# A three-tile pool of their own for the sums of a Strassen block's weights

## The chip, the cores and the metric

The kernel runs on one core of one Trainium2 chip. The metric is the device time of one execution in microseconds (us), lower is better. A core has a matrix engine (TensorE, PE in the profile, with its weight loads as PEld), a vector engine (VectorE, DVE), an activation engine (ScalarE, ACT), a general engine (GpSimd, POOL) and a queue engine that issues transfers (SyncE, SP). The engines run their own instruction streams in order and wait for each other by semaphores.

## The reference, cut to what matters

One layer of a decoder runs over 512 prompt positions and 8 x 4 sample positions, 544 columns in all. It ends in a feed-forward part, and the change concerns that part alone:

```
h2 = _rmsnorm(x, norm2_g) * (1 + sc2) + sh2
u1, u2 = jnp.split(h2 @ w_up, 2, axis=-1)          # w_up: 1024 x (2 x 2816)
x = x + g2 * ((jax.nn.silu(u1) * u2) @ w_down)     # w_down: 2816 x 1024
```

All values are float32. The part ahead of it (gated linear attention, windowed attention, gates and an output projection) is unchanged in what it computes.

## The kernel before

Activations lie feature by feature: a tile is 128 features x 544 columns (half a tile, 272 columns, is one matmul's width). A float32 product is made of three matmuls: each operand is split into a high part (a cast, on ACT) and a low part (the difference, on DVE), and the program sums hi*hi, hi*lo and lo*hi.

**Memory.** Almost every tile is taken from one pool, `heap`, of 62 slots of 128 x 544 floats. When a tile is no longer used, its slot goes back; the next tile takes a slot that was given back earlier, and its first writer waits until the slot's last users are done. Weights arrive by SP's queue in pieces of 128 x 2048 (`raw`, three buffers) and are split into pairs of 128 x 1024 tiles (`hi`, `lo`, three buffers each). `heap2` is a pool of 14 further slots that is opened when the feed-forward part starts, for the low and high parts of the operand sums TC below.

**The feed-forward part.** The program fixes each engine's order as it is written (there is no scheduler). The 22 output blocks of `w_up` (a u1 and a u2 block of 128 columns each) are made in two ways. Blocks 0 to 2 are plain products (`fm_pair`, L498). Blocks 3 to 21 are Strassen-Winograd products: seven products of half size, w1 to w7, in place of eight. They need

- sums of activations, once: `combos` (L1756), called for q = 0 to 3. Each makes four vector sums (L1761 on POOL, L1762, L1764 and L1766 on DVE) and splits them (`split`, L518: cast L521 on ACT, difference L522 on DVE) into the TC tiles;
- sums of weights, for each block: `s_sums` (L1779). POOL adds and subtracts the four 128 x 512 quarters of the block's `raw` piece in four instructions, L1784 to L1787, and leaves three sums in tiles S[0], S[1], S[2]; the fourth result is written over a quarter of `raw`. Below, "the sums of block n" are these four instructions.

The weights are then split by `s_pair` (cast L1796 on ACT, difference L1797 on DVE): `s_a` splits two raw quarters (for w1, w2), `s_b` splits S[0] and S[1] (w5, w6), `s_c` splits S[2] and the changed quarter (w3, w7), and `s_d` (L1813) the last quarter (w4, L1817 and L1818). `s_run` (L1849) goes through the blocks in three groups. The groups are blocks 3 to 8, 9 to 16 and 17 to 21. While block n's products run on PE in the order w2, w5, w6, w3, w7, then block n+1's w1 (`s_first`), then n's w4, the next block's weights are prepared, in this order: `s_sums(n+1)` ahead of everything, `s_a(n+1)` behind w2, `s_d(n)` behind w5, `s_b(n+1)` behind w6, `s_c(n+1)` behind w7. Each product has 12 matmuls (L1831). w4 is summed onto the same PSUM bank as w7 and may only start when DVE has read w7's result (L1876).

Ahead of the first group, `ffn` (L1888) interleaves the plain products of blocks 0 to 2 with the four `combos` and calls `s_sums(3)`. Behind each group stands the product with `w_down` (`down`).

Of the kernel before, what the change touches and what calls it, by code (L numbers as in the profile page):

```python
# [6 lines left out]
F32 = mybir.dt.float32  # L7
# [49 lines left out]
def ffn_order():  # L57
    seq = []
    f = 3
    for i, g in enumerate(GROUPS):  # L60
        top = min(g[-1] + 1, KF - 1)
        while f <= top:
            seq.append(("S", f))
            f += 1
        seq.append(("D", i))
    return seq
# [15 lines left out]
def prep(inp):  # L82
# [7 lines left out]
    def slab(w):  # L90
        k, n = w.shape
        return w.reshape(k // 128, 128, n).transpose(1, 0, 2).reshape(128, -1)
# [28 lines left out]
    for kind, i in ffn_order():  # L121
        if kind == "S":
            a1, a2 = slab(up("u1", i)), slab(up("u2", i))
# [205 lines left out]
class Body:  # L329
# [278 lines left out]
    def run(self):  # L608
        nc, tc, I, O = self.nc, self.tc, self.I, self.O
        with ExitStack() as es:  # L610
            P = lambda **k: es.enter_context(tc.tile_pool(**k))
            self.cp = P(name="const", bufs=1)
            self.sm = P(name="small", bufs=2)
            self.heap = P(name="heap", bufs=62)
            self.rawp = P(name="rawp", bufs=3)
            self.hip = P(name="hip", bufs=3)
            es.enter_context(tc.manual_schedule())
            with ExitStack() as em:
                Q = lambda **k: em.enter_context(tc.tile_pool(**k))
                self.kvp = Q(name="kvp", bufs=2)  # L620
                self.cm = Q(name="cmid", bufs=1)
                self.startup()
                with ExitStack() as ep:
                    self.psd = ep.enter_context(tc.tile_pool(name="psd", bufs=4, space=PSUM))
                    self.pmm = ep.enter_context(tc.tile_pool(name="pmm", bufs=2, space=PSUM))
                    self.mixers()
                    self.mid()
                self.psd = P(name="psf", bufs=8, space=PSUM)
                self.pmm = None
            self.heap2 = P(name="heap2", bufs=14)  # L630
            self.nheap2 = 14
            self.ffn()

    def startup(self):
# [205 lines left out]
    def gla_head(self, hd):  # L840
# [26 lines left out]
        v = lambda j: self.v[hd // 2][j][:, 256 * (hd % 2):256 * (hd % 2) + 256]  # L867
        S = {}
        us = [self.sd(), self.sd()]
        st = [self.t2("S"), self.t2("S")]  # L870
        o = lambda j: slice(256 * (j % 2), 256 * (j % 2) + 256)
        for j in range(4):
            nc.tensor.matmul(us[j // 2][:, o(j)], lhsT=klt[:, 128 * j:128 * j + 128], rhs=v(j), start=True, stop=True)
        for j in range(4):
# [3 lines left out]
            else:  # L878
                nc.vector.scalar_tensor_tensor(out=t, in0=S[j], scalar=self.fac[:, hd, 0, 2 * j:2 * j + 1],
                                               in1=u, op0=ALU.mult, op1=ALU.add)  # L880
            S[j + 1] = t
        self.store(self.O["sp"][hd], S[4], 2)
# [896 lines left out]
    def s_sums(self, n):  # L1779
        nc = self.nc  # L1780
        raw = self.s_raw(n)
        seg = [raw[:, 512 * i:512 * i + 512] for i in range(4)]
        S = [self.t2("S")[:, :512] for _ in range(3)]
        nc.gpsimd.tensor_add(S[0], seg[0], seg[3])  # L1784
        nc.gpsimd.tensor_sub(S[1], S[0], seg[1])
        nc.gpsimd.tensor_sub(seg[0], seg[1], seg[0])
        nc.gpsimd.tensor_sub(S[2], seg[2], S[1])  # L1787
        self.S[n] = S
# [53 lines left out]
    def s_first(self, n):  # L1842
# [4 lines left out]
        self.open[n] = (a, c, t)  # L1847

    def s_run(self, run, after):  # L1849

        nc = self.nc
        for n, nxt in zip(run, run[1:] + [None]):
            if nxt:
                self.s_sums(nxt)
# [33 lines left out]
    def ffn(self):  # L1888
# [76 lines left out]
        for j, (run, g) in enumerate(runs):  # L1965
            self.pos += 16 * len(run)

            def after():
                self.nchunk = self.pos // 8
                self.w_split(self.nchunk)  # L1970

            self.s_run(run, after)
            if j + 1 < len(runs):
                self.down(g, runs[j + 1][0][0])
            else:
                self.h2 = self.TC = None
                self.down_last(g)
# [113 lines left out]
```

## Time and profile before

| what | value |
|---|---|
| time, median of three runs | 1056.63 us (1056.44 to 1057.69) |
| the profiled execution's own time, its span | 1055.36 us, 1053.6 us |
| PE busy | 1014.9 us (96% of the span) |
| DVE, ACT, POOL busy | 580.4, 424.9, 269.7 us |
| DMA, mean share of 16 engines, read and written | 45% in the large queue, 143.8 and 36.6 MB |

The span runs from the first to the last instruction of the profiled execution; 1.8 us of its time lie outside. PE is the engine that has least idle time, so what counts is where PE waits, and for whom. The feed-forward part begins at about 650 us. In the kernel's views, "idle before" or a number in square brackets is the time that an engine waited ahead of an instruction and the instruction that released it.

### The profile page before, as it was taken

What the parts mean: (1) busy time and instruction counts of PE and PEld (TensorE: products, weight loads), DVE (VectorE), ACT (ScalarE), POOL (GpSimd) and SP (SyncE); (2) the same over time, 40 slices, a digit from 0 to 9 for tenths busy, and PEclk for the clock granted to TensorE, in tenths of its full rate; (3) what the DMA queues carried; (4) which work ended last, traced back from release to release, by engine and by line L of the source; (5) the groups of instructions that cost most, each with busy time, mean ns of one, the idle gap of its engine ahead of it and who ended that gap; (6) DMA issues with size and microseconds to landing.
All of it is one profiled execution on the core that took longest, in us unless ns stands there. A gap on an engine that the chain in (4) does not pass through costs nothing.

```text
span 1053.6 us, 21620 instructions
## 1 busy us (share of the span) xinstructions
PE 1014.9 (96%) x9309; PEld 954.5 (91%) x9309; DVE 580.4 (55%) x950; ACT 424.9 (40%) x728; POOL 269.7 (26%) x272
## 2 busy tenths in 40 slices
PE   8999999999999999999999999979999999999996
PEld 6898789999889999998989999879999999999995
DVE  6654424433452476353225767888734897447755
ACT  5452114554426422632043335455521655215553
POOL 0103004442332000200011431826114452044112
PEclk9999999999999999999999999989999999999997
DMA  9846572432133427725886572124473332322202
GB/s 366 329 137 254 204 269 98 176 128 85 59 116 118 161 91 264 270 81 168 294 295 219 187 212 108 41 91 159 169 302 140 141 120 81 121 80 81 90 32 85
DMA packets 47991, 169.21 MB, mean 161 GB/s; under 512 B 4044, under 2 KB 26924, under 8 KB 32412
## 3 DMA queue, kind: packets, MB, share of 16 engines
q1 hardware_dynamic: 47208, 166.90, 44.7%
q8 instruction: 73, 1.20, 0.5%
q10 hardware_dynamic: 688, 0.93, 0.3%
q14 instruction: 22, 0.18, 0.1%
HBM read 143.76 MB, written 36.63 MB: 171 GB/s over the span
## 4 chain that ended last, share of the span: by engine, by line
PE 85%; DVE 8%; ACT 3%; issue 3%; DMA 1%; POOL 1%; DVEq 0%; ACTq 0%; POOLq 0%
PE sd L1831 16%; PE mm L492 11%; PE mm L496 10%; PE mm L494 10%; PE sd L492 4%; PE sd L494 4%; PE sd L496 4%; PE mm L1026 3%; PE mm L1028 2%; PE mm L1027 2%; DVE lo L1797 2%; PE sd L538 2%; PE sd L1005 1%; PE sd L1406 1%; DVE lo L440 1%
## 5 line engine op out<-in xcount | busy, mean ns | idle before, releaser
L492 PE MATMUL mm<-hh,hi 128*128 128x272 f32 x656 | 139.3, 294 | 1.4 <-DVE gk L762 1.1
L496 PE MATMUL mm<-hh,lo 128*128 128x272 f32 x656 | 136.1, 289 | 1.2 <-DVE lo L440 1.2
L494 PE MATMUL mm<-hl,hi 128*128 128x272 f32 x656 | 135.7, 288 | 0.0
L440 DVE TENSOR_TENSOR lo<-raw,hi 128x1024 fp32r<-128x1024 f32 x92 | 115.1, 1252 | 35.7 <-ACT hi L439 35.3
L439 ACT CAST hi<-raw 128x1024 fp32r<-128x1024 f32 x92 | 95.3, 1046 | 76.6 <-PE sd L494 45.3
L492 PEld LDWEIGHTS mm<-hh,hi 128*128 128x128 f32 x656 | 102.7, 188 | 7.8 <-issue 3.1
L496 PEld LDWEIGHTS mm<-hh,lo 128*128 128x128 f32 x656 | 102.7, 188 | 1.5 <-DVE lo L440 1.4
L494 PEld LDWEIGHTS mm<-hl,hi 128*128 128x128 f32 x656 | 103.1, 189 | 0.0
L1784 POOL TENSOR_TENSOR S<-raw 128x512 f32<-128x512 f32 x19 | 29.0, 1529 | 188.6 <-DMA raw<-in_wst_dram 127.2
L1831 PE MATMUL sd<-h2h,hi 128*128 128x272 f32 x228 | 66.7, 292 | 5.5 <-ACT hi L1796 5.5
L1831 PE MATMUL sd<-h2h,lo 128*128 128x272 f32 x228 | 66.5, 292 | 0.4 <-DVE lo L1797 0.4
L1831 PE MATMUL sd<-h2l,hi 128*128 128x272 f32 x228 | 66.3, 291 | 0.0
L1831 PE MATMUL sd<-tch,lo 128*128 128x272 f32 x228 | 65.7, 288 | 0.0
L1831 PE MATMUL sd<-tcl,hi 128*128 128x272 f32 x228 | 65.5, 287 | 0.0
L1831 PE MATMUL sd<-tch,hi 128*128 128x272 f32 x228 | 65.4, 287 | 0.0
L492 PE MATMUL sd<-acth,hi 128*128 128x272 f32 x304 | 63.0, 288 | 0.0
L494 PE MATMUL sd<-actl,hi 128*128 128x272 f32 x304 | 62.8, 288 | 0.0
L496 PE MATMUL sd<-acth,lo 128*128 128x272 f32 x304 | 62.8, 288 | 0.0
L1099 ACT ACTIVATE qs<-mm,ca 32x544 f32<-32x544 f32 x48 | 33.9, 706 | 59.2 <-PE mm L496 53.9
L1470 ACT ACTIVATE sg<-mm,ca 128x544 f32<-128x544 f32 x16 | 11.4, 715 | 100.9 <-PE mm L496 92.4
L1797 DVE TENSOR_TENSOR lo<-S,hi 128x512 fp32r<-128x512 f32 x57 | 45.1, 820 | 9.9 <-ACT hi L1796 9.2
L1026 PE MATMUL mm<-hi,hh 128*128 128x512 f32 (+1 forms) x128 | 49.0, 383 | 0.0
(390 smaller groups left out, 2634.6 us busy)
## 6 DMA issues: line engine op xcount, KB each, us to landing
raw<-in_wst_dram SPq DMA_DIRECT2D x70, 1024.0 KB, 5.0
ada<-in_wada_dram SPq DMA_DIRECT2D x24, 1024.0 KB, 8.1
out_rest_dram<-in_rest_dram SPq DMA_DIRECT2D x16, 768.0 KB, 7.5
out_kn_dram<-kg SPq DMA_DIRECT2D x5, 1024.0 KB, 6.0
x<-in_xT_dram SPq DMA_DIRECT2D x16, 272.0 KB, 5.0
kg<-in_kg_dram SPq DMA_DIRECT2D x4, 1032.0 KB, 9.3
s<-in_s_dram SPq DMA_DIRECT2D x4, 1024.0 KB, 5.3
vg<-in_vg_dram SPq DMA_DIRECT2D x4, 1024.0 KB, 5.4
```

The costliest lines, as they stand in the source:

```text
L439: self.nc.scalar.copy(hi, src)
L440: self.nc.vector.tensor_sub(lo, src, hi)
L492: nc.tensor.matmul(outs[h], lhsT=wh, rhs=xh[:, h * NH:(h + 1) * NH], start=first, stop=False)
L494: nc.tensor.matmul(outs[h], lhsT=wh, rhs=xl[:, h * NH:(h + 1) * NH], start=False, stop=False)
L496: nc.tensor.matmul(outs[h], lhsT=wl, rhs=xh[:, h * NH:(h + 1) * NH], start=False, stop=last)
L538: nc.tensor.matmul(pa[32 * j:32 * j + 32, :64].rearrange("p (t i) -> p t i", t=2), lhsT=self.csil[:, 32 * k:32 * k + 32], rhs=wk[:, :, j, ...
L1026: nc.tensor.matmul(out(tt), lhsT=xh, rhs=wh, start=(k == 0), stop=False)
L1027: nc.tensor.matmul(out(tt), lhsT=xh, rhs=wl, start=False, stop=False)
L1099: nc.scalar.activation(self.two(qs)[32 * q:32 * q + 32], ps[32 * s:32 * s + 32, :, :NH], AF.Identity, bias=b[32 * s:32 * s + 32])
L1784: nc.gpsimd.tensor_add(S[0], seg[0], seg[3])
L1797: self.nc.vector.tensor_sub(lo[:, c:c + w], s, hi[:, c:c + w])
L1831: nc.tensor.matmul(out, lhsT=a[:, w], rhs=b, start=first and k == 0 and j == 0, stop=last and k == 3 and j == 2, skip_group_check=True)
```

## The change

The S tiles no longer come from `heap`. A pool `spool` with three tiles of 128 x 512 is opened with the feed-forward part, and `s_sums` takes S[0], S[1], S[2] from it for each block. To make room, `heap` has 61 slots in place of 62, and `heap2` 12 in place of 14, so that the last two sums of `combos`, rather than the last one, are split into `heap` tiles.

```diff
-            self.heap = P(name="heap", bufs=62)
+            self.heap = P(name="heap", bufs=61)
...
-            self.heap2 = P(name="heap2", bufs=14)
-            self.nheap2 = 14
+            self.spool = P(name="spool", bufs=3)
+            self.heap2 = P(name="heap2", bufs=12)
+            self.nheap2 = 12
...
-        S = [self.t2("S")[:, :512] for _ in range(3)]
+        S = [self.spool.tile([128, 512], F32, tag="S", name="S_%d" % self.bump()) for _ in range(3)]
```

On all five engines the instructions stand in the same order as before, and they do the same work; line numbers from L630 on are one higher. What differs is what some of them wait for. On POOL these are the sums of blocks 3, 4 and 5 before, each with the semaphores that it waits for (PE_49, DVE_49, Pool_49 count the instructions done on an engine, the DMAHW ones transfers landed):

```order
L1784 TENSOR_TENSOR S_7741<-raw_7515 128x512 [waits DMAHW0_49,PE_49]
L1785 TENSOR_TENSOR S_7742<-S_7741,raw_7515 128x512 [waits PE_49,Pool_49]
L1786 TENSOR_TENSOR raw_7515<-raw_7515 128x512 [waits DMAHW5_49]
L1787 TENSOR_TENSOR S_7743<-raw_7515,S_7742 128x512 [waits DVE_49,Pool_49]
L1784 TENSOR_TENSOR S_7788<-raw_7786 128x512 [waits DMAHW1_49,PE_49]
L1785 TENSOR_TENSOR S_7789<-S_7788,raw_7786 128x512 [waits PE_49,Pool_49]
L1786 TENSOR_TENSOR raw_7786<-raw_7786 128x512 [waits DMAHW6_49,DVE_49]
L1787 TENSOR_TENSOR S_7790<-raw_7786,S_7789 128x512 [waits PE_49,Pool_49]
L1784 TENSOR_TENSOR S_7925<-raw_7833 128x512 [waits DMAHW2_49,DVE_49]
L1785 TENSOR_TENSOR S_7926<-S_7925,raw_7833 128x512 [waits DVE_49,Pool_49]
L1786 TENSOR_TENSOR raw_7833<-raw_7833 128x512 [waits DMAHW7_49,DMAHW4_49,DVE_49]
L1787 TENSOR_TENSOR S_7927<-raw_7833,S_7926 128x512 [waits DVE_49,Pool_49]
```

And the same twelve of the changed kernel:

```order
L1785 TENSOR_TENSOR S_7744<-raw_7518 128x512 [waits DMAHW0_49]
L1786 TENSOR_TENSOR S_7745<-S_7744,raw_7518 128x512 [waits Pool_49]
L1787 TENSOR_TENSOR raw_7518<-raw_7518 128x512 [waits DMAHW5_49]
L1788 TENSOR_TENSOR S_7746<-raw_7518,S_7745 128x512 [waits Pool_49]
L1785 TENSOR_TENSOR S_7791<-raw_7789 128x512 [waits DMAHW1_49,DVE_49]
L1786 TENSOR_TENSOR S_7792<-S_7791,raw_7789 128x512 [waits DVE_49,Pool_49]
L1787 TENSOR_TENSOR raw_7789<-raw_7789 128x512 [waits DMAHW6_49]
L1788 TENSOR_TENSOR S_7793<-raw_7789,S_7792 128x512 [waits DVE_49,Pool_49]
L1785 TENSOR_TENSOR S_7928<-raw_7836 128x512 [waits DMAHW2_49,DVE_49]
L1786 TENSOR_TENSOR S_7929<-S_7928,raw_7836 128x512 [waits DVE_49,Pool_49]
L1787 TENSOR_TENSOR raw_7836<-raw_7836 128x512 [waits DMAHW7_49,DMAHW4_49]
L1788 TENSOR_TENSOR S_7930<-raw_7836,S_7929 128x512 [waits DVE_49,Pool_49]
```

Before, block 4's sums waited for matmuls, the last users of the heap slots that they got. Now the wait of the sum S[i] of block n+1 on DVE is for the difference (L1797, now L1798) of block n's S[i], the last reader of the same buffer: S[0] and S[1] follow `s_b(n)`, S[2] follows `s_c(n)`. For block 3 there is nothing to wait for but its transfer.

## Rows read from the trace of the kernel before

**Rows 1.** Waits of PE from 640 us on: total, times, longest.

```profile
PE sd L1831 <- ACT hi L1796: 5.5, 1, 5.5
PE sd L1831 <- DVE u L1876: 4.6, 6, 1.0
...
PE sd L492 <- ACT hi L439: 1.3, 1, 1.3
PE sd L496 <- DVE lo L440: 1.0, 1, 1.0
```

**Rows 2.** PE in order of time: start, us, operation, [idle before it].

```profile
697.44 0.59 PE L1831 MATMUL sd<-h2h,hi 128*128 128x272 f32 x1 [5.49 <-ACT hi L1796]
...
710.42 0.29 PE L1831 MATMUL sd<-tch,wh 128*128 128x272 f32 x1
...
732.79 0.39 PE L1831 MATMUL sd<-tch,wh 128*128 128x272 f32 x1 [0.99 <-DVE u L1876]
```

**Rows 3.** ACT in order of time, a cast of 128x1024.

```profile
681.79 1.04 ACT L439 CAST hi<-raw 128x1024 fp32r<-128x1024 f32 x1
```

**Rows 4.** DVE in order of time, 677 to 696 us.

```profile
677.22 1.55 DVE L522 TENSOR_TENSOR tcl<-ta,tch 128x544 fp32r<-128x544 f32 x1 [0.18 <-ACT tch L521]
678.70 1.81 DVE L522 TENSOR_TENSOR tcl<-tb,tch 128x544 fp32r<-128x544 f32 x1
...
681.91 1.56 DVE L522 TENSOR_TENSOR actl<-su,acth 128x544 fp32r<-128x544 f32 x1 [0.71 <-ACT acth L521]
683.39 1.21 DVE L440 TENSOR_TENSOR lo<-raw,hi 128x1024 fp32r<-128x1024 f32 x1
...
686.78 0.72 DVE L522 TENSOR_TENSOR tcl<-tb,tch 128x544 fp32r<-128x544 f32 x1
687.42 0.50 DVE L1762 SCALAR_TENSOR_TENSOR tb<-h,dB,h 128x272 f32<-128x272 f32 x1
...
689.68 1.81 DVE L522 TENSOR_TENSOR tcl<-tb,tch 128x544 fp32r<-128x544 f32 x1
691.42 1.50 DVE L1762 SCALAR_TENSOR_TENSOR tb<-h,dB,h 128x272 f32<-128x272 f32 x1
...
694.38 1.39 DVE L1766 SCALAR_TENSOR_TENSOR tb<-h,B,ta 128x272 f32<-128x272 f32 x1
```

**Rows 5.** POOL in order of time: block 4's first sum, block 5's first and last.

```profile
676.90 1.29 POOL L1784 TENSOR_TENSOR S<-raw 128x512 f32<-128x512 f32 x1 [0.70 <-DMA raw<-in_wst_dram]
...
689.60 1.31 POOL L1784 TENSOR_TENSOR S<-raw 128x512 f32<-128x512 f32 x1 [6.71 <-DMA raw<-in_wst_dram]
...
694.01 1.46 POOL L1787 TENSOR_TENSOR S<-raw,S 128x512 f32<-128x512 f32 x1
```

**Rows 6.** DVE in order of time, block 3 of the first group.

```profile
702.31 1.90 DVE L1797 TENSOR_TENSOR lo<-S,hi 128x512 fp32r<-128x512 f32 x3 [1.53 <-ACT hi L1796]
...
707.37 1.29 DVE L1797 TENSOR_TENSOR lo<-S,hi 128x512 fp32r<-128x512 f32 x2 [0.47 <-ACT hi L1796]
...
709.11 0.44 DVE L1876 TENSOR_TENSOR u<-sd,s 128x272 f32<-128x272 f32 x1
```

**Rows 7.** Groups of DVE instructions from 640 us: count, busy us, mean ns.

```profile
L1859 DVE TENSOR_TENSOR su<-sd,sA 128x272 f32<-128x272 f32 x19 | 8.2, 430 | 0.0
```

**Rows 8.** Busy time by stretch: PE, PEld, DVE, ACT, POOL, granted clock, DMA.

```profile
694.80:701.70 6.90, 3.82 (x15) 3.50 (x16) 4.97 (x7) 2.78 (x6) 0.67 (x1) 0.51 0.00 0
```

**Rows 9.** DVE in order of time, during block 12's products.

```profile
854.10 2.38 DVE L1797 TENSOR_TENSOR lo<-S,hi 128x512 fp32r<-128x512 f32 x2
```

**Rows 10.** POOL in order of time, beside rows 9.

```profile
848.36 1.30 POOL L1784 TENSOR_TENSOR S<-raw 128x512 f32<-128x512 f32 x1 [3.92 <-DVE lo L1797]
...
853.58 1.74 POOL L1787 TENSOR_TENSOR S<-raw,S 128x512 f32<-128x512 f32 x1
```

**Rows 11.** The pm tiles: loads and readers, count, ns, first to last start.

```profile
L367 SPq DMA_DIRECT2D pm<-in_cb_dram x2: 328/534/741, 434.9 to 443.5; - x2
L1365 DVE TENSOR_TENSOR pn<-pm,sd x2: 677/680/682, 458.7 to 459.3; 96x512 f32<-96x512 f32 x2
```

## Prediction

> **What bounds the kernel now.** PE is busy for 96% of the span, so a change can gain only where PE waits. I read the waits of PE from the feed-forward part on first: one wait of 5.5 us for a cast of ACT (L1796), six of 4.6 us together for L1876 on DVE, and two smaller ones for the split of a chunk (L439, L440) [rows 1]. In order of time the long one stands at 697.44, ahead of w1 of block 3, the first Strassen product; the longest of the six stands at 732.79, ahead of w4 of block 5 [rows 2].
>
> Then I follow the long wait back. The cast that ends it has the shape of the one at 681.79, which takes 1.04 us [rows 3], so it begins at about 696.4. On ACT it stands behind the casts of the last `combos`, which need the sums that DVE makes between 689.68 and 695.77 (694.38 + 1.39). What to see there is DVE's own durations: the same split (L522, 128x544) takes 0.72 at 686.78 and 1.81 at 689.68, the same sum (L1762) 0.50 at 687.42 and 1.50 at 691.42; the row left out behind it is a second sum of 1.50 [rows 4]. POOL's rows say why: block 5's four sums run from 689.60 to 695.47, block 4's four from 676.90 on [rows 5]. A DVE instruction that reads two SBUF tiles ends 0.3 to 0.6 us after the POOL instruction under way (678.77 after 678.19) [rows 4, 5]. So PE waits for a chain on DVE and ACT, and sums on POOL that nobody needs for another 10 us lengthen that chain.
>
> **The change, part by part.**
>
> *Block 4's and 5's sums move.* With three S tiles, block 4's first sum waits for the difference of block 3's S[0], the first of the three at 702.31, which lies behind w1 of block 3; block 5's waits for block 4's, at 707.37 [rows 6]. Both leave the stretch ahead of 697.44. What DVE gets back, by rows of the same shape without POOL beside them: 677.22, 678.70 and 681.91 lose 0.83, 1.09 and 0.84, together 2.76; 689.68 loses 1.09, and the three sums of 128x272 behind it 1.00, 1.00 and 0.89, together 3.98 [rows 4].
>
> How much of it arrives at 697.44? The difference at 683.39 also needs its cast. With DVE 1.92 earlier, the cast begins at 681.79 - 1.92 = 679.87, ends at 680.9, and the difference follows, 2.4 earlier than before [rows 3, 4]. I take 2.4 of the 2.76. From there DVE and ACT alternate up to 689 without a wait for PE or a transfer, so the 2.4 is carried; the 3.98 is added in full, since ACT's casts stand directly behind these sums. PE then begins block 3 at 697.44 - 6.4 = 691.0. Its plain products ended at 691.95 (697.44 - 5.49) [rows 2]; of their own waits of 1.3 and 1.0 for that chunk [rows 1] at least 1.7 goes, so they end by 690.3 and are no new bound. Term: **-6.4**. Bounds: -4.0 (the first part is lost) and -6.7 (all of both).
>
> *The granted clock.* Behind the long wait the granted clock is 0.51 from 694.8 to 701.7, the lower of the two levels (1.2 GHz) [rows 8]. PE works in 4.3 us of that; at the upper level it would need at most 2.1 less. The wait that is left is about 3 us, still long, so I keep the cost: term 0, bounds -2.1 and +1.0.
>
> *What is given back.* Block 4's sums now run from about 702.99 - 6.4 = 696.6 on, beside DVE's work for block 3: the differences of S[1], S[2], of raw pieces, and of block 4's S[0] and S[1]. The trace has no sums of POOL there, so I price it by its nearest rows: each of the four POOL instructions holds back one difference by up to 1.09, 4.4 in all [rows 4]. Who waits is L1876 of block 3, which is queued behind them on DVE; w4 may not start ahead of it. DVE has 0.47 idle at 707.37, and L1876 ends at 709.55 [rows 6], 0.87 before PE comes to w4 at 710.42 [rows 2]. So PE loses 4.4 - 0.5 - 0.9 = 3.0. Bounds: 0 (POOL gets its turn only in DVE's gaps) and 6.4 (the whole gain). Term: **+3.0**.
>
> Here it matters which DVE instructions are held back. L1859, L1873 and L1876 read one operand from PSUM. L1859 stands right ahead of a long difference, in the stretch where POOL adds; its 19 have a mean of 430 ns and 8.2 us together [rows 7], so none is long. The Trainium skill says the same ("SBUF — State Buffer", section "Who interferes with whom"): a VectorE instruction with at most one SBUF input does not contend with GpSimd, one with two does, and the later one waits for the whole of the other. The trace agrees with both halves. If PSUM readers were held back too, L1873 and L1876 would cost another 2.2 at block 3.
>
> *The other blocks.* Sixteen blocks have a successor in their group. Before, POOL is two blocks ahead: it adds when a raw piece has landed, for instance from 848.36 to 855.32 [rows 10], right beside `s_b`'s pair of differences, which takes 2.38 at 854.10 [rows 9] against 1.29 at 707.37 [rows 6]. L1876 stands behind that pair. Afterwards POOL begins when S[0]'s difference is done, so that this pair and what stands ahead of it on DVE run free, 1.1 us earlier or more, and POOL meets what stands behind: L1877, S[2]'s difference, the changed quarter's, the next `act`. PE needs none of these within the next product. So I expect the waits of w4 for L1876 inside a group to go: three of the six (the 0.99 at 732.79 stands for them [rows 2]). The other three stand at the last block of a group, where no w1 lies between w7 and w4, and stay. Three of 0.8 to 1.0 are about 2.5; I take **-2.0**, bounds -2.6 and 0. The sums stay in time: the next block needs them a block later, 10.7 us (two blocks lie between 710.42 and 732.79, less the 0.99 [rows 2]), and four take 5.9 to 7.0 [rows 5, 10].
>
> *One heap slot and two slots of `heap2` fewer.* No instruction is added; a tile gets a slot that was given back one tile later. The longest delay that I find is SP's first pm load: issued at 434.9, it may have to wait as long as the second, to 443.5. Nothing is queued between the two, and they are read at 458.7, 15 us on [rows 11]; without that cover the 8.6 would be paid. Term 0, bounds 0 and +1.
>
> Sum: -6.4 + 3.0 - 2.0 = **-5.4**. Against the profiled execution's own 1055.36 that is 1050.0; the runs have a median 1.27 above it, so the forecast is 1056.63 - 5.4 = **1051.2 us**.
>
> **Rivals.**
>
> *Cleaner:* nothing is given back, and the clock stays up after the shorter wait: -6.4 - 2.1 - 2.0, 1046.1. For it: DVE issues back to back there. Against: POOL got its turn between DVE's instructions in every stretch shown. Chance 0.13.
>
> *Given back at once:* block 4's sums, made late, also hold up `s_b(4)`. The pair that reads S[0] and S[1] begins at 707.37 - 6.4 = 701.0 [rows 6], its cast some 0.5 earlier (half of the 1.04 [rows 3]), at 700.5; the two sums, begun at 696.6, need 3.0 to 3.5. With 0.4 to 0.9 of slack it can happen; the whole 6.4 may go, and only the -2.0 counts: 1054.6 to 1056.6. Chance 0.11.
>
> *Slower, three tiles are too few:* every block's sums wait for the differences of the block before. If the four, taking turns with DVE, needed over 13 us in place of 7, each of the 16 would be late for `s_c` and PE would wait for the excess; at 0.5 us each that is +8, less the 3.4 that the start keeps: 1061. The trace speaks against it by a factor of two [rows 10]. The Trainium skill has the rule that speaks for it ("Perfetto Trace Analysis", section "Optimization Strategy"): a gap that repeats on the engine that should be saturated can mean too few buffers. No run here shows such a gap on PE yet. Chance 0.07.
>
> *The change does nothing:* the cast ahead of 697.44 is held by something that comes just behind DVE. The rows show no such thing, and ACT's work there is short. Chance 0.03, within 1 us of before.
>
> **How the numbers follow.** The forecast has 0.66; its own range is 1048.5 to 1054. A difference below 0.2% (2.1 us) is about what a measurement of this kernel can't tell from none. Faster: 0.66, 0.13 and a third of the 0.11: 0.83. Same: the rest of the 0.11 and the 0.03: 0.10. Slower: 0.07. The range for 8 in 10 leaves out half of the cleaner case, the slower one and the upper end of the second: 1047.0 to 1056.0.
>
> **What would show it.** POOL: no sums between 677 and 696, block 4's first right behind block 3's S[0] difference. DVE: L522 at 0.72 and L1762 to L1766 at 0.50 in the last `combos`. PE: idle ahead of block 3 near 3 us, not 5.49; a new wait of 2 to 4 us for L1876 at w4 of block 3; no wait inside groups. It would be wrong if DVE's rows were long there without POOL beside them, if ACT's L1796 waited for POOL in each block, or if L1876 took longer than 0.44.

## The result, and the profile after

| what | before | after |
|---|---|---|
| time, median of four runs | 1056.76 us (1056.44 to 1057.69) | 1045.58 us (1044.85 to 1046.29) |
| ratio, 95% interval | | 0.9898 (0.9883 to 0.9912) |
| profiled execution, its span | 1055.36, 1053.6 us | 1045.04, 1043.3 us |
| PE busy | 1014.9 us (96%) | 1011.5 us (97%) |

The change gains 11.2 us where 5.4 were forecast; five more runs gave 0.9902 (0.9885 to 0.9919). The two profiles of the changed kernel show less, 10.3 and 8.0 us of span, since the profiled execution of the kernel before was 1.4 us faster than its median, and the second profile is of the slowest of its five runs. The instructions are the same, so the two traces can be laid beside each other matmul by matmul. The table gives how much earlier (-) or later (+) PE does each stretch, from the starts of the same matmuls; times of places are those of before.

| stretch | forecast | first profile | a second one |
|---|---|---|---|
| ahead of 640 us | 0 | -1.6 | 0.0 |
| 640 to 697.5: start of block 3 | -6.4 | -6.6 | -6.4 |
| 697.5 to 720: blocks 3 and 4 | +3.0 | +2.4 | +3.0 |
| 720 to 1040: the other blocks | -2.0 | -4.6 | -4.6 |

The cut at 697.5 lies behind block 3's first matmul. Cut at the start of that matmul, the second and third rows are -6.4 and +2.2 in the first profile, -6.4 and +3.0 in the second.

First the waits of PE from 640 us on, after the change (total, times, longest). Lines from L630 on are one higher, so L1877 is what was L1876 and L1797 what was L1796 in [rows 1].

```profile
PE sd L1832 <- DVE u L1877: 3.4, 4, 1.4
PE sd L1832 <- ACT hi L1797: 3.0, 1, 3.0
...
PE sd L1832 <- DVE lo L1798: 0.7, 1, 0.7
```

The wait of 5.5 for the cast is 3.0; the waits of 1.3 and 1.0 for L439 and L440 are no longer in the list. Four waits for DVE's read of w7 are left. In order of time, PE at the start of block 3 and at its w4, the places of [rows 2]:

```profile
689.49 0.39 PE L1832 MATMUL sd<-h2h,hi 128*128 128x272 f32 x1 [3.00 <-ACT hi L1797]
...
690.75 0.40 PE L1832 MATMUL sd<-h2h,lo 128*128 128x272 f32 x1 [0.74 <-DVE lo L1798]
...
704.20 0.39 PE L1832 MATMUL sd<-tch,wh 128*128 128x272 f32 x1 [1.37 <-DVE u L1877]
```

Block 3 starts at 689.49, 7.95 ahead of 697.44, of which 1.6 were there before 640 us; 704.20 is the new wait at w4. POOL in order of time:

```profile
694.40 1.67 POOL L1785 TENSOR_TENSOR S<-raw 128x512 f32<-128x512 f32 x1 [19.71 <-DVE lo L1798]
...
699.43 2.27 POOL L1788 TENSOR_TENSOR S<-raw,S 128x512 f32<-128x512 f32 x1
...
846.25 1.67 POOL L1785 TENSOR_TENSOR S<-raw 128x512 f32<-128x512 f32 x1 [4.00 <-DVE lo L1798]
```

There is no sum between 677 and 694.4, where there were eight [rows 5]; block 4's begin when DVE has made the difference of S[0]. Inside a group they begin when the first difference of the pair that they ran beside in [rows 9, 10] is done (846.25, in the pair that began at 845.47). DVE in order of time:

```profile
675.70 0.72 DVE L522 TENSOR_TENSOR tcl<-ta,tch 128x544 fp32r<-128x544 f32 x1 [0.18 <-ACT tch L521]
676.34 0.72 DVE L522 TENSOR_TENSOR tcl<-tb,tch 128x544 fp32r<-128x544 f32 x1
...
686.36 0.49 DVE L1763 SCALAR_TENSOR_TENSOR tb<-h,dB,h 128x272 f32<-128x272 f32 x1
...
693.62 2.99 DVE L1798 TENSOR_TENSOR lo<-S,hi 128x512 fp32r<-128x512 f32 x3 [0.79 <-ACT hi L1797]
696.54 1.78 DVE L1798 TENSOR_TENSOR lo<-raw,hi 128x512 fp32r<-128x512 f32 x1
698.24 0.43 DVE L1860 TENSOR_TENSOR su<-sd,sA 128x272 f32<-128x272 f32 x1
698.59 1.96 DVE L1798 TENSOR_TENSOR lo<-raw,hi 128x1024 fp32r<-128x1024 f32 x1
700.48 1.77 DVE L1819 TENSOR_TENSOR wl<-raw,wh 128x512 fp32r<-128x512 f32 x1
...
703.73 0.42 DVE L1877 TENSOR_TENSOR u<-sd,s 128x272 f32<-128x272 f32 x1
...
845.47 1.29 DVE L1798 TENSOR_TENSOR lo<-S,hi 128x512 fp32r<-128x512 f32 x2 [0.51 <-ACT hi L1797]
```

The splits of `combos` take 0.72 in place of 1.55 and 1.81 and its sums 0.49 in place of 1.50 [rows 4]. What they have shed stands from 694.8 to 702: the last of the three differences at 693.62 (2.99 in place of 1.90 [rows 6]) and those at 696.54, 698.59 and 700.48 run beside block 4's sums, ahead of the read of w7 at 703.73. The PSUM reader at 698.24, between two of them, takes its 0.43 as ever [rows 7]. The pair at 845.47 is the one that stood at 854.10: 1.29 in place of 2.38 [rows 9].

The granted clock behind the shorter wait, in the first profile and then in a second one of the same kernel (busy time by stretch: PE, PEld, DVE, ACT, POOL, clock, DMA, as in [rows 8]):

```profile
691.70:695.10 3.40, 3.40 (x17) 3.40 (x16) 2.20 (x4) 2.79 (x6) 0.70 (x1) 0.50 0.00 0
```

```profile
691.20:696.50 5.30, 4.86 (x20) 4.54 (x21) 3.06 (x6) 2.19 (x5) 0.00 (x0) 0.50 0.00 0
```

PE still falls to the lower level, for 3.4 us in the one and at least 5.3 in the other. That length differs between executions of one kernel, and it is most of the difference between +2.4 and +3.0 in the table: from block 3's first matmul to the one ahead of its w4 PE loses 0.2 us in the first profile and 0.7 in the second.

### The profile page after: what moved, and what is told of

Its sections match the earlier page's. It is cut to its first block, busy times and chain, and to the rows that moved or that the text cites. A ratio compares the mean times of both kernels' runs of the same rounds, so it can differ in the third digit from the quotient of the medians.

```text
span 1043.3 us, 21634 instructions
## 1 busy us (share of the span) xinstructions
PE 1011.5 (97%) x9309; PEld 954.1 (91%) x9309; DVE 575.1 (55%) x950; ACT 423.6 (41%) x728; POOL 270.6 (26%) x272
## 4 chain that ended last, share of the span: by engine, by line
PE 85%; DVE 6%; issue 3%; ACT 3%; POOL 1%; DMA 1%; DVEq 0%; POOLq 0%; ACTq 0%
PE sd L1832 17%; PE mm L492 11%; PE mm L494 10%; PE mm L496 10%; PE sd L492 4%; PE sd L494 4%; PE sd L496 4%; PE mm L1027 2%; PE mm L1029 2%; PE mm L1028 2%; PE sd L538 2%; DVE lo L1798 1%; DVE lo L440 1%; PE sd L1407 1%; PE acc L492 1%
## 5 line engine op out<-in xcount | busy, mean ns | idle before, releaser
L440 DVE TENSOR_TENSOR lo<-raw,hi 128x1024 fp32r<-128x1024 f32 x92 | 115.0, 1251 | 36.8 <-ACT hi L439 36.3
L439 ACT CAST hi<-raw 128x1024 fp32r<-128x1024 f32 x92 | 95.3, 1045 | 76.5 <-PE sd L494 45.3
L1785 POOL TENSOR_TENSOR S<-raw 128x512 f32<-128x512 f32 x19 | 33.0, 1739 | 178.7 <-DVE lo L1798 103.9
L1798 DVE TENSOR_TENSOR lo<-S,hi 128x512 fp32r<-128x512 f32 x57 | 52.9, 957 | 11.0 <-ACT hi L1797 10.9
L1798 DVE TENSOR_TENSOR lo<-raw,hi 128x1024 fp32r<-128x1024 f32 (+1 forms) x38 | 53.6, 1411 | 0.1
```

The source lines that it names most:

```text
L439: self.nc.scalar.copy(hi, src)
L440: self.nc.vector.tensor_sub(lo, src, hi)
L1798: self.nc.vector.tensor_sub(lo[:, c:c + w], s, hi[:, c:c + w])
```

## The experiments

Each ran four to twelve times beside the kernel before on the same chip (the runs of one table are not all from one chip), and has one profile. **Theory A**: only the moment of POOL's sums counts; they hold back DVE instructions that read two SBUF tiles. **Rival B**: the S tiles out of the heap let other tiles find slots sooner. **Rival C**: the time ahead of 640 us comes from the heap of 61 slots. All stretches are as in the table above.

| kernel | ratio (95%) | to 640 | start | blocks 3, 4 | others |
|---|---|---|---|---|---|
| changed, second time | 0.9902 (0.9885 to 0.9919) | 0.0 | -6.4 | +3.0 | -4.6 |
| wait alone, all blocks | 0.9928 (0.9916 to 0.9941) | +1.2 | -6.6 | +3.1 | -4.5 |
| wait, blocks 4 and 5 | 0.9994 (0.9985 to 1.0003) | +2.1 | -6.6 | +3.1 | +2.6 |
| wait, from block 6 on | 0.9957 (0.9940 to 0.9974) | +1.7 | -1.0 | +1.0 | -4.5 |
| before, heap 61 | 0.9997 (0.9988 to 1.0006) | -0.8 | 0.0 | +0.6 | +0.5 |
| changed, heap 62 | 0.9923 (0.9911 to 0.9936) | +0.1 | -6.6 | +3.1 | -4.5 |
| the same again | 0.9926 (0.9913 to 0.9938) | +0.1 | -6.6 | +3.1 | -4.4 |
| six tiles | 0.9986 (0.9974 to 0.9998) | 0.0 | -4.0 | +2.6 | +2.1 |
| eight additions put back | 0.9967 (0.9956 to 0.9978) | -1.0 | -3.5 | +5.7 | -4.6 |
| memsets put back | 0.9913 (0.9894 to 0.9933) | -1.7 | -6.2 | +3.0 | -4.6 |

**The wait without the pool.** The heap stays at 62 slots, the S tiles stay in it; a write of one column into the previous block's S[0] makes POOL wait for its readers.

```diff
+        if n > 3:
+            nc.gpsimd.memset(self.old[:, :1], 0.0)
+        self.old = S[0]
         nc.gpsimd.tensor_add(S[0], seg[0], seg[3])
```

> The kernel before with its heap as it was and no pool of S tiles. Ahead of each block's sums POOL writes one column of the previous block's S[0], so that the sums wait for the difference (on DVE) of that S[0], as with three tiles. Theory A (only the moment of POOL's sums counts): start of block 3 earlier by 6.6, about 2.0 given back at w4 of blocks 3 and 4, 4.6 gained at w4 inside the groups: -9.2 us, near 1047.4. Rival B (the slots do it: with the S tiles out of the heap other tiles find free slots sooner): within 1 us of before, 1056.7. Rival C (the 1.4 us ahead of 640 us comes from the heap of 61 slots): as A, and nothing changes ahead of 640 us.

Measured -7.6 us (0.9928 of 1055.8), 1.6 less than expected: by its profile 3.1 is given back at blocks 3 and 4, not 2.0, and 1.2 is lost ahead of 640 us. From 640 us on its stretches are those of the changed kernel, without pool or fewer slots: rival B falls. In the profiles the rest of the gap to the changed kernel lies ahead of 640 us (+1.2 against -1.6 and 0.0).

**The wait for some blocks only**: the same with `n in (4, 5)`, and with `n > 5`.

> The same one-column write ahead of the sums of blocks 4 and 5 alone; from block 6 on POOL may run ahead as before. Theory A: start of block 3 earlier by 6.6, the give-back of 2.0 stays, the waits at w4 inside the groups stay: -4.6 us. If the give-back needs later blocks' sums too, -6.6. Rival B: 0 within 1 us.

> The one-column write ahead of the sums of block 6 and later alone; blocks 4 and 5 add early, as before. Theory A, as the first four runs left it (the gain at w4 inside the groups comes from sums that wait for the previous block's differences, and stands apart from the start of block 3): the start of block 3 stays at 697.4 and the waits of w4 from 732.79 on go: -3.5 to -4.6 us. If these waits went only because the first blocks had been moved, 0.

The second came as expected (-4.5 us by 0.9957). Its -1.0 and +1.0 around block 3's start show how much hangs on the moment: block 5's first sum begins at 691.48 there, just behind the start of the split (L522) at 691.46, and that split takes 0.72 where it took 1.81 before. Of the 1.0, PE loses 0.6 again in its next wait, for the difference of w1's weights (1.04 in place of 0.44), and 0.4 in a lower clock that ends later. The first did not: -0.6 by its ratio, though block 3 starts 6.6 earlier. Its trace, POOL, DVE and PE in order of time:

```profile
713.80 1.83 POOL L1787 TENSOR_TENSOR S<-raw 128x512 f32<-128x512 f32 x1
...
719.53 1.71 POOL L1790 TENSOR_TENSOR S<-raw,S 128x512 f32<-128x512 f32 x1
```

```profile
718.34 3.45 DVE L1800 TENSOR_TENSOR lo<-S,hi 128x512 fp32r<-128x512 f32 x2
```

```profile
722.55 0.39 PE L1834 MATMUL sd<-tch,wh 128*128 128x272 f32 x1 [2.76 <-DVE u L1879]
```

Block 6's sums, which nothing holds, follow block 5's at once, the pair of block 5 takes 3.45 in place of 1.29, and w4 of block 4 waits 2.76. So the gain at the start is kept only because the later blocks' sums wait too. My expectation had added up the places as if they were independent.

**How many tiles.** A pool of its own, with six tiles (`bufs=6`, `heap2` with 10).

> The changed kernel with six S tiles in the pool in place of three (and 10 slots of heap2 in place of 12), so that sums wait for the differences of the block before the previous one. Theory A (what counts is that POOL is held back): block 4's sums run early again at 677, block 5's do not; of the 6.6 at the start about 4 stay, 1.6 or more is given back at blocks 3 and 4, the waits of w4 inside the groups are back, and the 1.1 of the heap of 61 slots stays: -2 to -4 us against before. If a pool of their own is what helps, whatever its size: -10.

-1.5 us (0.9974 to 0.9998), where -2 to -4 were expected: the other blocks don't only keep their waits, they lose 2.1 more than before. POOL and the waits of PE from 640 us on:

```profile
676.63 1.53 POOL L1785 TENSOR_TENSOR S<-raw 128x512 f32<-128x512 f32 x1 [0.46 <-DMA raw<-in_wst_dram]
...
699.06 1.67 POOL L1785 TENSOR_TENSOR S<-raw 128x512 f32<-128x512 f32 x1 [16.21 <-DVE lo L1798]
```

```profile
PE sd L1832 <- DVE u L1877: 8.3, 9, 1.1
```

Block 4's sums run early again and block 5's do not: of the 6.6, 4.0 stay, about what the forecast gave to block 5's sums (3.98). With two blocks' tiles POOL runs ahead again and w4 waits nine times. The small number of tiles is what helps.

**What holds DVE back.** The changed kernel, with eight POOL instructions in the places of the eight that had moved; then with memsets (and one copy) in place of each four additions.

```diff
+        r = self.s_raw(4)
+        for i in range(8):
+            if i == 4:
+                self.nc.gpsimd.tensor_copy(out=self.scr[:, :1], in_=self.TC[2][-1][:, :1].bitcast(F32))
+            q = r[:, 512 * (i % 4):512 * (i % 4) + 512]
+            self.nc.gpsimd.tensor_add(self.scr, q, r[:, :512])
```

> The changed kernel, and POOL does eight idle additions of 128x512 into a tile that nobody reads, four when block 4's piece has landed (about 677) and four behind the last difference of the third combos (about 687). They stand ahead of block 4's sums on POOL and nothing waits for their result. Theory A (two readers of SBUF, DVE and POOL, take turns): block 3 starts 6.4 to 7.5 us later than in the changed kernel, the rest stays: 1052 to 1053 us. If the early start came from a wait for slots, 0: 1045.6.

> As the run before, but POOL only writes: one copy and eight memsets of 128x512 in place of each four additions. If POOL's mere occupation of SBUF or its writing held DVE back, block 3 starts some 6 us later, as there. If it is its reading beside DVE's: 1 us or less (the two copies read), near 1046 us.

From 640 to 720 us PE loses 6.4 against the first profile of the changed kernel with the additions, 0.9 with the memsets (5.7 and 0.2 against the second). POOL, DVE and the waits of PE with the additions:

```profile
675.76 5.99 POOL L1797 TENSOR_TENSOR scr<-raw 128x512 f32<-128x512 f32 x4 [0.56 <-DMA raw<-in_wst_dram]
...
689.81 6.02 POOL L1797 TENSOR_TENSOR scr<-raw 128x512 f32<-128x512 f32 x4
```

```profile
677.45 1.81 DVE L522 TENSOR_TENSOR tcl<-tb,tch 128x544 fp32r<-128x544 f32 x1
...
691.21 1.79 DVE L522 TENSOR_TENSOR tcl<-ta,tch 128x544 fp32r<-128x544 f32 x1
...
694.64 2.28 DVE L1806 TENSOR_TENSOR lo<-raw,hi 128x1024 fp32r<-128x1024 f32 x1
```

```profile
PE sd L1840 <- ACT hi L1805: 3.6, 1, 3.6
...
PE sd L1840 <- DVE lo L1806: 3.2, 1, 3.2
```

The time came out as expected (1052.0), but not in the way expected: block 3 starts only 3.1 later than in the changed kernel (-3.5 against -6.6), not 6.4 to 7.5. The second four additions begin at 689.81, when DVE is three instructions further than it was when block 5's sums began in the kernel before, so that the last sums of `combos` are held back less and what follows them more. The difference of w1's weights at 694.64 takes 2.28 (1.23 in the kernel before), and PE waits 3.2 for it, just behind block 3's start.

And with the memsets:

```profile
676.46 0.53 POOL L1800 MEMSET scr<- 128x512 f32 x1
...
688.35 0.53 POOL L1800 MEMSET scr<- 128x512 f32 x1
```

```profile
676.31 0.71 DVE L522 TENSOR_TENSOR tcl<-tb,tch 128x544 fp32r<-128x544 f32 x1
...
687.94 0.72 DVE L522 TENSOR_TENSOR tcl<-ta,tch 128x544 fp32r<-128x544 f32 x1
```

L522 takes 1.8 beside additions and 0.72 beside memsets: POOL's reading holds it back, its writing does not. The run with memsets has this twice over: its two copies of 128x512, which read, stretch the DVE instructions beside them a little (L522 to 0.87, a sum of `combos` to 0.73), its memsets none. The Trainium skill says so ("SBUF — State Buffer", section "Who interferes with whom"): two SBUF inputs on VectorE contend with a GpSimd instruction that reads SBUF, not with one that only writes it. The two runs agree (1.8 and 0.72 us).

**61 or 62 slots.** The kernel before with `bufs=61`, and the changed kernel with `bufs=62`, the latter twice.

> The kernel before with 61 heap slots in place of 62, everything else as it was. Theory A: 0 within 0.5 us. Rival C (the other slots of tiles ahead of 640 us are worth the 1.4 us seen there): -1.4 us, all of it ahead of 640 us. The forecast's term was 0 to +1.

> The changed kernel with 62 heap slots as before; the three S tiles and the 12 slots of heap2 stay. Theory A: as the changed kernel, 1045.6 within 0.5 us. Rival C: 1.4 us slower than the changed kernel, 1047.0, with the loss ahead of 640 us. Rival B (a scarcer heap makes the difference): between the two.

> The changed kernel with 62 heap slots, beside the changed kernel on the same chip. If the ACT table load that stands behind a wait for PE at 443.2 with 62 slots, and runs ahead of it with 61, is worth the 1.1 us: 1 to 1.5 us slower than the changed kernel, with the wait of 1.2 for a split at 452.7. If the 61 slots do nothing: the same within 0.5 us.

> The changed kernel itself once more, beside the next three on one chip: ratio 0.988 to 0.991, as first measured. What of its 10 us is not at the start of block 3, at its give-back or at w4 inside groups (about 1.1 at 452.7) should be seen in its trace again.

On one chip 0.9902 stands against 0.9926: 2.5 us, but the two intervals overlap, so the timing alone doesn't settle it. In all eighteen profiles one row agrees: PE's wait of 1.2 for L440 at 452.7 is in each of the six with 62 slots, and in none of the twelve with 61. ACT in order of time there, before (the wait that ends at 443.20 is for PE), then after:

```profile
443.20 1.28 ACT L1470 ACT_TABLE_LOAD   x1 [5.21 <-PE mm L496]
444.50 0.72 ACT L1470 ACTIVATE sg<-mm,ca 128x544 f32<-128x544 f32 x1
```

```profile
437.29 1.28 ACT L1471 ACT_TABLE_LOAD   x1
443.12 0.71 ACT L1471 ACTIVATE sg<-mm,ca 128x544 f32<-128x544 f32 x1 [4.55 <-PE mm L496]
```

The sigmoid at L1470 takes its output tile from the heap. With 62 slots that is a slot which POOL used last. The sigmoid then waits for POOL and for PE's product; in the program the wait for POOL stands on the sigmoid and the one for PE on the load of its table, ahead of it. With 61 slots it gets another slot, has one wait, and the load runs 6 us early, during ACT's idle time. Everything behind it on ACT comes 1.3 earlier, up to the split at 452.7. PE, before:

```profile
452.70 0.52 PE L496 MATMUL mm<-hh,lo 128*128 128x272 f32 x2 [1.19 <-DVE lo L440]
```

So rival C holds for 1.1 us: the start-to-start time of that matmul falls from 1.47 to 0.37. At 640 us PE is 0.7 earlier than in the kernel before on the mean of the twelve profiles with 61 slots, 0.9 later on that of the six with 62; of these 1.5 us the 1.1 is the part with a cause. The rest of what a single profile shows ahead of 640 us (-1.7 to +2.1) goes with neither number of slots: it stands in the first 30 us and in stretches where the granted clock differs between executions (0.50 to 0.58 from 316 to 320, 0.87 to 0.93 from 426 to 452, in four kernels). The kernel before gains nothing in all from 61 slots (0.9997); its trace gives the gain back in waits of w4 (nine in place of six, 5.6 us) and in clock at block 3.

**The waits that are left.** Three of 0.69 us stand at the last block of a group, where no w1 lies between w7 and w4; one of 1.4 to 1.6 at block 3's w4. I tried to take them out of the changed kernel.

| kernel | ratio (95%) | start | blocks 3, 4 | others |
|---|---|---|---|---|
| w7 ahead of w3 in last blocks | 0.9898 (0.9883 to 0.9914) | -6.4 | +3.0 | -5.3 |
| and split of block 4's S[0], S[1] later | 0.9921 (0.9907 to 0.9935) | -6.6 | +4.3 | -5.3 |
| w2, w6, w5, w7, w3, w4 in last blocks | 0.9910 (0.9894 to 0.9927) | -6.3 | +3.0 | -3.8 |
| and the chunk's split behind w7's read | 0.9890 (0.9873 to 0.9908) | -6.6 | +2.4 | -7.4 |
| half of block 4's sums later | 0.9893 (0.9878 to 0.9908) | -6.5 | +2.3 | -4.4 |
| third and fifth row together | 0.9909 (0.9894 to 0.9924) | -6.4 | +2.4 | -3.6 |

> The changed kernel; in the last block of each group w7 runs ahead of w3, so that w3's 12 matmuls (1.5 us) lie between w7 and w4 while DVE reads w7's result. The three waits of w4 that the change left there (0.69 us idle each, about 0.95 from start to start) go: -2.5 to -3 us against the changed kernel, if its waits are for L1877 behind w7 alone. If DVE is late there for other reasons: 0.

> The changed kernel; in the last block of each group the products run in the order w2, w6, w5, w7, w3, w4, so that one product lies between any two that add to the same PSUM bank. If the three waits at the groups' ends are the reads between w6, w7 and w4 alone, all go, and none takes their place as w7's did two runs ago: -2.5 to -3 us against the changed kernel. If DVE or ACT is late there anyway: 0.

> The order w2, w6, w5, w7, w3, w4 in the last block of each group, as three runs ago, and the split of the next chunk (cast, and a difference of 1.23 us on DVE), which stood ahead of DVE's read of w7 there, moved behind it. If that difference in DVE's queue is why w4 still waited: the three waits at the groups' ends go, -2.5 to -3 us against the changed kernel, 1042 us. If the product with w_down then waits for the chunk that is split later: 0, and the waits stand behind the groups.

The first swap only moved the read: PE now waits at w7 for ACT's copy of w6's result, 1.4 us in three waits, and only 0.2 is gained in each of the three blocks (-5.3 in place of -4.6).

```profile
PE sd L1832 <- ACT sA L1867: 1.4, 3, 0.5
```

With every pair of products on one bank separated, the waits at w4 did not go; they grew by 0.26 each. DVE, in the first of these blocks:

```profile
757.24 1.23 DVE L440 TENSOR_TENSOR lo<-raw,hi 128x1024 fp32r<-128x1024 f32 x1 [0.57 <-ACT hi L439]
758.38 0.43 DVE L1879 TENSOR_TENSOR u<-sd,s 128x272 f32<-128x272 f32 x1
```

The read of w7 (L1879 here) stood behind the split of the next chunk (L440). With that behind the read all three waits are gone.

```diff
             if not nxt:
                 self.s_mm(n, 7, a, False)
                 nc.vector.tensor_add(u[:, NH:], a, s5[:, :NH])
+                after()
             self.s_mm(n, 3, c, False)
...
-            else:
-                after()
```

The trace shows -2.8 against the changed kernel in the other blocks, three times 0.95, as expected. It is the fastest median (1043.32 us), but its interval overlaps that of the changed kernel, so the gain is shown in the trace and not in the timing.

> As the run before, and in block 3 alone the split of block 4's S[0] and S[1] moves from ahead of DVE's read of w7 to behind it. If the give-back of 2.0 at blocks 3 and 4 comes from DVE's queue ahead of that read (S differences held back by block 4's sums): another -1.5 to -2 us. If block 4's w5 then waits for that split: 0 or some us slower.

> The changed kernel; of block 4's four sums the third and fourth wait for the difference of block 4's S[0] (a one-column write into it holds POOL back) instead of running beside the two long differences ahead of DVE's read of w7. If the give-back at blocks 3 and 4 is these two differences (1.96 and 1.77 us against 1.23 and 0.69 alone), DVE reads w7 1.8 us earlier and the wait of 1.4 to 1.6 at block 3's w4 goes: -1.5 to -2 us against the changed kernel. If block 4's split of S[2] is late instead: 0 or slower.

> Both edits at once. If they are independent, as the two places 50 us apart say: -4 to -5 us against the changed kernel, 1040 to 1041 us.

Moving the split behind DVE's read lost: w3 of block 4 waits 2.8 for ACT. Holding back the third and fourth sum of block 4 did what was expected of it on DVE:

```profile
699.86 1.21 DVE L1805 TENSOR_TENSOR lo<-raw,hi 128x1024 fp32r<-128x1024 f32 x1
701.00 0.68 DVE L1826 TENSOR_TENSOR wl<-raw,wh 128x512 fp32r<-128x512 f32 x1
...
706.17 1.12 DVE L1805 TENSOR_TENSOR lo<-S,hi 128x512 fp32r<-128x512 f32 x1 [1.84 <-ACT hi L1804]
```

The two differences take 1.21 and 0.68 in place of 1.96 and 1.77, and the wait at block 3's w4 is gone: from start to start 0.29 in place of 1.65. But S[2] is late, DVE sits 1.84 waiting for its cast, and w3 of block 4 waits for ACT:

```profile
PE sd L1839 <- ACT s L1871: 1.4, 1, 1.4
```

1.26 of the 1.37 came back there. The give-back is the held-back differences, and it can't be removed by moving half of the sums; the two edits together gave no more than either.

## Why the prediction was right or wrong

The direction and the mechanism were right. The time, 1045.6, lies 5.6 us below the forecast and 1.4 below the range for 8 in 10 (1047.0): two terms were mis-sized.

**Block 4's and 5's sums move (-6.4): right, -6.4 by block 3's first matmul in both profiles.** The two parts are shown apart: with six tiles block 4's sums are back and 4.0 stay (forecast 3.98). With idle additions near both places the gain is lost by 720 us, about half of it at the start and most of the rest in the next wait.

**The granted clock (0) and the give-back (+3.0): right together, +2.2 and +3.0, in part by luck.** Four differences were held back as forecast, by 1.09, 1.09, 0.73 and 1.08 (alone they take 0.69, 0.69, 1.23 and 0.69 in other rows), 4.0 in all and not 4.4; less the 1.4 of slack that the forecast took off, 2.6 should be lost up to w4. In the second profile 2.6 are: 0.7 in the lower clock, 1.9 at w4 (1.6 of it idle, where a wait of 2 to 4 had been named as the sign). The wait at w4 ends when DVE has read w7, so what the clock takes ahead of it is not waited for again; the forecast had counted the two one by one. In the first profile the clock stayed up until 691.7 and only 1.8 are lost, 0.2 and 1.6; the copy that ACT makes of w1's result came earlier, and DVE's idle time ahead of the three differences fell from 1.53 [rows 6] to 0.79, in the second profile to 1.52. Another 0.4 is lost in both at block 4's w3, which the forecast had not priced; that it makes up for the 0.4 too much in the differences is luck.

**The other blocks (-2.0, bounds -2.6 and 0): the step that failed; it measured -4.6.** The mechanism is right: POOL begins when the pair's first difference is done, and the waits inside groups go, while those at the last blocks stay (here 0.69 each). Two errors made the term small. First, I priced a wait by its idle time. PE's next matmul starts 0.125 us after the last when it need not wait, but a matmul's own row is 0.29 long, and idle time counts from its end. At 732.79 the idle time is 0.99 [rows 2], the start-to-start time 1.27 where 0.13 would do, and the next matmul is 0.1 late as well: 1.26 lost. The rows on either side of that wait, and a wait that the list does not have, in the kernel before:

```profile
731.52 0.29 PE L1831 MATMUL sd<-h2h,lo 128*128 128x272 f32 x1
...
733.02 0.29 PE L1831 MATMUL sd<-tcl,wh 128*128 128x272 f32 x1
...
856.84 0.29 PE L1831 MATMUL sd<-h2h,lo 128*128 128x272 f32 x1
857.23 0.39 PE L1831 MATMUL sd<-tch,wh 128*128 128x272 f32 x1
```

The first of these two places in the changed kernel:

```profile
725.62 0.29 PE L1832 MATMUL sd<-h2h,lo 128*128 128x272 f32 x1
725.74 0.29 PE L1832 MATMUL sd<-tch,wh 128*128 128x272 f32 x1
```

The three waits that I counted cost 1.26, 1.04 and 1.06, together 3.4. Second, there are waits so short that the list leaves them out: at 857 to 879 three starts are 0.31 to 0.38 apart in place of 0.13, and each of the three loses 0.29 to 0.37, at 721 and 744 another 0.18 and 0.16. That makes 1.3, and with the 3.4 the whole of the 4.6. The profile showed it all, in starts and not in idle times. All eight are gone in the changed kernel; the run with the wait alone, and the one with the wait from block 6 on, have the same -4.5 there, so it is the later sums that do it.

**One heap slot fewer (0, bounds 0 and +1): wrong in sign, -1.1 at 452.7**. The timing of 61 against 62 slots puts it at about 2.5, with intervals that overlap, the mean of the profiles at 1.5; a cause is shown for the 1.1 alone. I had looked for waits that a slot given back later could add, and not for one that another slot could remove.

**The rivals.** "Cleaner" comes nearest in time (1046.1), for other reasons: something is given back and the clock does fall. "Given back at once" is not seen in the changed kernel. Its time is what came out when only blocks 4 and 5 were made to wait, but by another way: block 6's sums beside DVE, not block 4's sums being late. "Three tiles are too few" is refuted: no wait for `s_c` inside a group is in the list, and six tiles are slower (0.9986 against 0.9898 and 0.9902). The rule of the Trainium skill that spoke for it ("Perfetto Trace Analysis", section "Optimization Strategy": a gap that repeats can mean too few buffers) is turned round by this trace: the gap at w4 repeats nine times with six tiles and four times with three.

Still open: what 61 slots give beyond the 1.1 at 452.7 (0.4 by the mean of the profiles, 1.4 by the timing), if it is there at all.

## What to carry to other kernels

Work that runs ahead of its need isn't free when it shares something with an engine on the path: a pool with few buffers is a cheap way to hold it back, and the next thing to look at is what stands beside it at its new place. Price a wait by the start-to-start time of the instruction that waited against that of its undisturbed neighbours, not by the idle time; three waits that the trace gives as 0.02 to 0.1 us idle held a microsecond here. When a pool changes size, compare what every instruction waits for, far from the change too.

## What was not expected of the hardware

- POOL's memsets of 128x512 (0.53 us) leave DVE's two-input instructions at their length (0.72), its additions (1.3 to 1.7) bring them to 1.8.
- A table load on ACT (1.28 us) can stand behind a wait that belongs to the activation after it: a second wait on an activation, for the last user of its output's slot, cost PE 1.1 us.
- Behind a wait of 3.0 us of PE the granted clock stood at 0.50 for 3.4 us in one execution and for at least 5.3 in another of the same kernel.
